# A hybrid decoder layer on one core: the rings of split weight chunks moved 128 bytes up in SBUF

## The chip, the cores and the metric

The kernel runs on one core of one Trainium2 chip. The metric is the device time of one execution in microseconds. The kernel before was timed in three runs: median 771.52 us, from 771.47 to 771.79. One further execution was recorded by the hardware profiler; its own time was 770.06 us, and from its first to its last instruction 768.3 us pass.

## The reference

One decoder layer over x of 256 tokens by 1024 channels, all in float32. Three sub-layers follow each other, each with an RMS norm ahead of it and behind it and a residual sum: a SwiGLU feed-forward of width 2816 with half weight; a mixer that runs a Mamba-2 branch (32 heads of 64, state 128, chunks of 128) beside a differential attention (8 heads) and merges the two with per-channel sigmoid gates; a second SwiGLU feed-forward.

```python
h = h + 0.5 * rmsnorm(swiglu(rmsnorm(h, g1), w_gate, w_up, w_down), g2)
z, xbc, dt, q, k, v, gates = split(rmsnorm(h, g3) @ w_in)
merged = sigmoid(gates_0) * ssd_branch(z, xbc, dt) + sigmoid(gates_1) * diff_attn_branch(q, k, v)
h = h + rmsnorm(merged @ w_out, g4)
h = h + 0.5 * rmsnorm(swiglu(rmsnorm(h, g5), w_gate2, w_up2, w_down2), g6)
```

Nearly all arithmetic is in the products with the weights, some 34 million float32 numbers that are read once.

## The kernel before, in words

**Split products.** Every large product is made from three products in a reduced float32 format: each operand is split into a high part (the operand rounded to that format) and a low part (what the rounding left), and high by high, low by high and high by low are summed. Activations are split once and stay in SBUF. Weights come in chunks of 128 partitions by 2048 numbers (1 MB, 8192 bytes in each partition). A chunk is loaded by SyncE's queue into a buffer named raw (line 217 on). ScalarE rounds it into whi (line 254), VectorE subtracts whi from raw into wlo (line 261), and TensorE multiplies with both.

**Rings.** The buffers of whi and wlo come from the function ring (line 195), one ring for each of the two. Each ring has three buffers in the pool sb, which lives as long as the kernel does. In the two feed-forward stages it has a fourth buffer in the pool of the stage: the ring counts its calls, and where the count modulo four is 3 the stage's buffer is given (line 201 on). In the mixing stage the counter still runs modulo four, but all buffers come from the three of sb. The chunks of the seven-product form of a feed-forward group (names whiq and wloq) go through the same rings. Two chunks at each border of two stages (seams, line 190) use small buffers of the stage's pool in place of the rings.

**Two kinds of products.** In mm_nat (line 386, its matmul is L395) and mm_n (line 596, L610) the weight chunk is the moving operand, 512 columns in each matmul, and a 128 by 128 block of the split activations is the stationary one. In mm_t (line 374, lines L381, L382 and L384) it is the other way round: a 128 by 128 block of whi or wlo is stationary and 256 columns of the split activations move. mm_t makes the convolution inputs, z, q and k of the mixing stage (28 chunks of 48 matmuls); the rest, both feed-forwards and the gates, branches and output of the mixing stage, is made by the other two. In a printed operand list "acc_f<-whi,gh_f" the first name behind the arrow is the moving operand.

**Order.** TensorE, ScalarE, VectorE and SyncE run in an order that is written out by hand in the feed-forwards (own_order, line 429 and 622); parts of the mixing stage are ordered by the framework, and from line 1374 on TensorE's order is by hand again. GpSimd is ordered by the framework throughout. Attention and the state-space recurrence run as background work between the matmuls of the mixing stage.

**Addresses.** Tiles of a pool lie one behind the other in the order in which their names are first used, each rounded up to 32 bytes. Pool const comes first, then sb, then the stage's pool. This is how the tiles lie in a partition of the program as it is built, in bytes; the last columns are the remainders by 256.

| tiles | pool | start before | start after the change | by 256 before | after |
|---|---|---|---|---|---|
| ident | const | 26,240 | 26,240 | 128 | 128 |
| raw, three buffers | sb | 30,624 | 30,624 | 160 | 160 |
| u0, u1 (activations of a norm, split; also o8) | sb | 55,200 | 55,200 | 160 | 160 |
| k2 (six work tiles) | sb | 71,904 | 71,904 | 224 | 224 |
| whi, three buffers | sb | 84,512 | 84,640 | 32 | 160 |
| wlo, three buffers | sb | 109,088 | 109,216 | 32 | 160 |
| small tiles | sb | 133,664 | 133,920 | | |
| stage pools: gh, gl, yh, mh, S, the fourth whi and wlo, two more raw buffers, and others | stage | 134,304 | 134,560 | 160 | 160 |

All blocks that the matmuls of whole chunks take out of these tiles start a multiple of 256 bytes from the tile's start, so the remainder of a tile is that of its operands.

Of the kernel before, what the change touches and what calls it, by code (L numbers as in the profile page):

```python
# [14 lines left out]
F32 = mybir.dt.float32  # L15
# [9 lines left out]
P = 128  # L25
T = 256
D = 1024
# [28 lines left out]
def tile_hybrid_layer(ctx: ExitStack, tc: tile.TileContext, x, ffn1_pre_g, ffn1_w_gate, ffn1_w_up,  # L56
# [4 lines left out]
    nc = tc.nc  # L61
    const = ctx.enter_context(tc.tile_pool(name="const", bufs=1))
    sb = ctx.enter_context(tc.tile_pool(name="sb", bufs=1))
# [122 lines left out]
    raws, pairs, taken, rings = [], {}, [0], {}  # L186
# [5 lines left out]
    def mixing(c):  # L192
        return mix_first <= c < mix_last

    def ring(kind, n, more, name, c, dt=F32):

        i = rings.get(kind, 0) % (n + more)
        rings[kind] = rings.get(kind, 0) + 1
        if i < n or stage[1][1] != FFN_K4 or mixing(c):
            return sb.tile([P, 2 * D], dt, tag=kind, name=name, bufs=n)  # L200
        return stage[1][0].tile([P, 2 * D], dt, tag=kind, name=name, bufs=more)

    class Raw:
# [32 lines left out]
    def blocks(name, c, nj, nc_):  # L236

        if c in seams:
            n = nj // 2
            ts = [k4([P, n, nc_], f"{name}{q}", F32R) for q in range(2)]  # L240
            return lambda j, m: ts[j // n][:, j % n:j % n + m, :]
        t = ring(name[:3], SPLIT_BUFS, SPLIT_MORE, name, c, F32R).rearrange("p (j c) -> p j c", j=nj)
        return lambda j, m: t[:, j:j + m, :]
# [226 lines left out]
    for name, v in (("mx", mix_pre_g), ("f2", ffn2_pre_g),  # L470
                    ("ng", ssd_norm_g), ("cb", ssd_conv_b), ("sg", da_subln_g)):
        n = v.shape[1] // P
# [540 lines left out]
    dt = const.tile(shp, F32, name="dt")  # L1013
# [488 lines left out]
```

## Time and profile before

| | |
|---|---|
| median of three runs | 771.52 us (771.47 to 771.79) |
| time of the profiled execution | 770.06 us |
| its span, first to last instruction | 768.3 us |
| TensorE matmul busy | 747.3 us, 97% |
| VectorE busy | 563.8 us, 73% |
| ScalarE busy | 430.8 us, 56% |
| GpSimd busy | 41.7 us, 5% |
| read from and written to HBM | 136.17 MB and 1.08 MB, 179 GB/s over the span |

The profile lists for each engine the time in which it has an instruction under way. Matmuls overlap: a matmul starts before the one ahead of it is through, and the ends are modelled, so the mean length of a matmul in a group is longer than the distance between two starts. The pace of TensorE is read from the starts.

### The profile page before, as it was taken

The page shows a single profiled execution, that of the slowest core. Times are in us where ns is not written, and L with a number is a line of the kernel's source. Part 1 is how long each engine was busy: PE and PEld are TensorE (multiplying, and loading weights), DVE is VectorE, ACT ScalarE, POOL GpSimd, SP SyncE. Part 2 cuts the span into 40 slices and gives each one's busy share as a digit, 9 for nine tenths or more (in the row PEclk, how much of TensorE's full clock was granted, in tenths as well). Part 3 has the DMA queues.
Part 4 walks back from the last instruction along what each step waited for, and adds up shares of the span by engine and source line. Part 5 has one row for each costly group of instructions (what it writes and reads, how often), then busy time and mean ns, then how long its engine had stood idle before and what let it go on. Part 6 is the DMA issues. An engine that isn't in the chain of part 4 may idle for free.

```text
span 768.3 us, 10269 instructions
## 1 busy us (share of the span) xinstructions
PE 747.3 (97%) x4113; PEld 628.5 (82%) x4113; DVE 563.8 (73%) x666; ACT 430.8 (56%) x583; POOL 41.7 (5%) x72
## 2 busy tenths in 40 slices
PE   8999899999989999999999999999999999999996
PEld 7877687788768999989999787787877888888885
DVE  6788897853557788777878878685777899987332
ACT  7543746733545555776966554774464647566321
POOL 6000000000141000000000000000012000000000
PEclk9999999999999999999999999999999999999999
DMA  9950845963355866664555564454564908458201
GB/s 324 309 194 0 275 164 169 335 208 136 103 131 177 264 188 175 188 188 141 165 180 178 151 205 140 162 165 164 165 220 164 319 10 275 162 187 334 108 1 55
DMA packets 77888, 137.92 MB, mean 179 GB/s; under 512 B 2748, under 2 KB 35600, under 8 KB 77840
## 3 DMA queue, kind: packets, MB, share of 16 engines
q1 hardware_dynamic: 75168, 129.51, 50.9%
q0 software_dynamic: 2368, 7.22, 3.2%
q8 instruction: 32, 0.52, 0.3%
q10 hardware_dynamic: 304, 0.53, 0.2%
q14 instruction: 16, 0.13, 0.1%
HBM read 136.17 MB, written 1.08 MB: 179 GB/s over the span
## 4 chain that ended last, share of the span: by engine, by line
PE 81%; DVE 7%; ACT 6%; issue 3%; POOL 1%; DMA 1%; SPq 0%; DVEq 0%; ACTq 0%; POOLq 0%
PE acc_f L610 15%; PE pu_f L395 6%; PE pg_f L395 5%; PE pws L395 5%; PE pgt L395 4%; PE pa_f L395 4%; PE pn_f L395 3%; ACT whi L254 3%; PE pwd L395 3%; DVE wlo L261 3%; PE pd_f L395 3%; PE pxs L382 2%; PE pxs L384 2%; PE pxs L381 2%; PE pz L382 2%
## 5 line engine op out<-in xcount | busy, mean ns | idle before, releaser
L261 DVE TENSOR_TENSOR wlo<-raw,whi 128x2048 fp32r<-128x2048 f32 (+2 forms) x116 | 243.5, 2109 | 96.1 <-ACT whi L254 94.0
L254 ACT CAST whi<-raw 128x2048 fp32r<-128x2048 f32 (+2 forms) x116 | 202.1, 1759 | 131.8 <-PE acc_f L610 39.5
L254 ACT CAST whiq<-raw 128x2048 fp32r<-128x2048 f32 x24 | 45.9, 1911 | 28.4 <-PE pu_f L395 11.8
L261 DVE TENSOR_TENSOR wloq<-raw,whiq 128x2048 fp32r<-128x2048 f32 x24 | 54.7, 2285 | 6.4 <-ACT whiq L254 6.4
L610 PE MATMUL acc_f<-whi,gh_f 128*128 128x512 f32 x160 | 52.3, 395 | 0.0
L610 PE MATMUL acc_f<-wlo,gh_f 128*128 128x512 f32 x160 | 52.0, 395 | 0.2 <-DVE wlo L261 0.2
L610 PE MATMUL acc_f<-whi,gl_f 128*128 128x512 f32 x160 | 52.1, 394 | 0.0
L610 PEld LDWEIGHTS acc_f<-wlo,gh_f 128*128 128x128 f32 x160 | 29.9, 188 | 7.5 <-DVE wlo L261 0.6
L610 PEld LDWEIGHTS acc_f<-whi,gl_f 128*128 128x128 f32 x160 | 30.0, 188 | 7.0
L395 PE MATMUL pgt<-whi,u_mx 128*128 128x512 f32 x128 | 35.5, 403 | 0.2 <-DVE gt L1406 0.2
L610 PEld LDWEIGHTS acc_f<-whi,gh_f 128*128 128x128 f32 x160 | 29.8, 188 | 6.8
L395 PE MATMUL pg_f<-whi,u_f 128*128 128x512 f32 x128 | 32.9, 399 | 0.9 <-DVE sg_f L768 0.9
L395 PE MATMUL pu_f<-whi,u_f 128*128 128x512 f32 x128 | 32.2, 394 | 0.0
L381 PE MATMUL pz<-u_mx,whi 128*128 128x256 f32 x128 | 31.9, 285 | 0.0
L382 PE MATMUL pz<-u_mx,whi 128*128 128x256 f32 x128 | 31.8, 285 | 0.0
L381 PE MATMUL pxs<-u_mx,whi 128*128 128x256 f32 x128 | 31.5, 284 | 0.0
L382 PE MATMUL pxs<-u_mx,whi 128*128 128x256 f32 x128 | 31.2, 282 | 0.0
L395 PEld LDWEIGHTS pg_f<-whi,u_f 128*128 128x128 f32 x128 | 23.5, 188 | 6.5 <-DVE sg_f L768 1.4
L395 PEld LDWEIGHTS pgt<-whi,u_mx 128*128 128x128 f32 x128 | 23.3, 188 | 6.6 <-issue 1.3
L395 PEld LDWEIGHTS pu_f<-whi,u_f 128*128 128x128 f32 x128 | 24.0, 188 | 5.5
L395 PE MATMUL pn_f<-whi,u_f 128*128 128x512 f32 x96 | 25.1, 395 | 0.0
L381 PEld LDWEIGHTS pz<-u_mx,whi 128*128 128x128 f32 x128 | 24.1, 189 | 0.5 <-issue 0.5
(371 smaller groups left out, 1648.3 us busy)
## 6 DMA issues: line engine op xcount, KB each, us to landing
raw<-in_w_in_dram SPq DMA_DIRECT2D x40, 1024.0 KB, 5.3
raw<-in_ffn_w_down_dram SPq DMA_DIRECT2D x22, 1024.0 KB, 5.3
raw<-in_ffn_w_gate_dram SPq DMA_DIRECT2D x18, 1024.0 KB, 5.5
raw<-in_ffn_w_up_dram SPq DMA_DIRECT2D x18, 1024.0 KB, 5.2
raw<-in_ssd_w_branch_dram SPq DMA_DIRECT2D x8, 1024.0 KB, 5.1
raw<-in_ffn_w_up_dram SPq DMA_DIRECT2D x8, 512.0 KB, 5.7
acb<-acd POOLq DMA_DIRECT2D x8, 512.0 KB, 5.0
raw<-in_da_w_branch_dram SPq DMA_DIRECT2D x4, 1024.0 KB, 5.1
```

Of the source, the lines that this page charges most:

```text
L254: i = nc.scalar.copy(got["hi"](j, step), src()[:, j:j + step, :])
L261: nc.vector.tensor_sub(got["lo"](j, step), src()[:, j:j + step, :], got["hi"](j, step).bitcast(F32))
L381: nc.tensor.matmul(acc[m], wh(j)[:, cs], ah(k0 + j), start=first and j == ks[0], stop=False)
L382: nc.tensor.matmul(acc[m], wh(j)[:, cs], al(k0 + j), start=False, stop=False)
L384: nc.tensor.matmul(acc[m], wl(j)[:, cs], ah(k0 + j), start=False, stop=last and j == ks[-1])
L395: nc.tensor.matmul(acc, a(k0 + j), b(j), start=first and i == 0, stop=last and i == 11, skip_group_check=go_on)
L610: nc.tensor.matmul(acc[b][q], x_[:, ts], w_(kt)[:, halves[q]], start=i == 0 and kt == 0 and x_ is ah and w_ is wh, stop=i == n - 1 and kt ...
```

## The change

A function gap makes a tile of 128 partitions by 32 float32 numbers (128 bytes in each partition) in pool sb and clears it with a GpSimd memset. It is called twice: just ahead of the first whi buffer and just behind the first wlo buffer. So whi and wlo start 128 bytes higher, and all that lies behind wlo, the small tiles and the stage pools, 256 bytes higher. Nothing reads the two tiles. The last byte used in a partition goes from 229,024 to 229,280.

```diff
+    def gap(name):
+        nc.gpsimd.memset(sb.tile([P, 32], F32, tag=name, name=name, bufs=1), 0.0)
+
     def ring(kind, n, more, name, c, dt=F32):
 
+        first = kind not in rings
         i = rings.get(kind, 0) % (n + more)
         rings[kind] = rings.get(kind, 0) + 1
         if i < n or stage[1][1] != FFN_K4 or mixing(c):
-            return sb.tile([P, 2 * D], dt, tag=kind, name=name, bufs=n)
+            if first and kind == "whi":
+                gap("gap0")
+            t = sb.tile([P, 2 * D], dt, tag=kind, name=name, bufs=n)
+            if first and kind == "wlo":
+                gap("gap1")
+            return t
         return stage[1][0].tile([P, 2 * D], dt, tag=kind, name=name, bufs=more)
```

## The prediction

> **What bounds the kernel now.** I read the page first: busy times, the slices over time, the chain that ended last.
>
> ```profile
> span 768.3 us, 10269 instructions
> PE 747.3 (97%) x4113; PEld 628.5 (82%) x4113; DVE 563.8 (73%) x666; ACT 430.8 (56%) x583; POOL 41.7 (5%) x72
> PE   8999899999989999999999999999999999999996
> PEclk9999999999999999999999999999999999999999
> PE 81%; DVE 7%; ACT 6%; issue 3%; POOL 1%; DMA 1%; SPq 0%; DVEq 0%; ACTq 0%; POOLq 0%
> ```
>
> TensorE is busy in nearly every slice at a full granted clock and carries 81% of the chain. So the time is set by how far apart its matmuls start. The second view is the busy time by stretches, for the place where another engine comes nearest.
>
> ```profile
> 60.00:100.00 40.00, 37.82 (x165) 29.57 (x164) 33.32 (x25) 22.07 (x17) 0.00 (x0) 1.00 0.49 159
> 260.00:320.00 60.00, 60.00 (x501) 59.67 (x500) 48.60 (x75) 32.77 (x41) 0.53 (x1) 1.00 0.62 186
> 620.00:680.00 60.00, 60.00 (x270) 48.90 (x269) 56.10 (x37) 32.91 (x29) 0.00 (x0) 1.00 0.43 146
> ```
>
> Columns: matmul, weight load, VectorE, ScalarE, GpSimd, then clock, share of the DMA engines and GB/s. Nobody else is full; VectorE reaches 56.1 of 60 us in the second feed-forward.
>
> Third, the order of time on TensorE alone, in the down projection of the first feed-forward. It has no background work and hardly a wait, and each chunk is 24 matmuls of 512 columns. The chunks that start at 157.26 and at 179.54 lie in the stage's fourth buffers (remainder 160 by 256), those that start at 162.75, 168.34 and 173.94 in the rings of sb (remainder 32). The stationary operands lie at remainder 160 throughout.
>
> ```profile
> 157.26 0.63 PE L610 MATMUL acc_f<-whi,gh_f 128*128 128x512 f32 x2
> ...
> 159.58 0.62 PE L610 MATMUL acc_f<-wlo,gh_f 128*128 128x512 f32 x2
> ...
> 162.30 0.62 PE L610 MATMUL acc_f<-wlo,gh_f 128*128 128x512 f32 x2
> 162.75 0.62 PE L610 MATMUL acc_f<-whi,gh_f 128*128 128x512 f32 x2
> ...
> 168.34 0.63 PE L610 MATMUL acc_f<-whi,gh_f 128*128 128x512 f32 x2
> ...
> 173.94 0.63 PE L610 MATMUL acc_f<-whi,gh_f 128*128 128x512 f32 x2
> ...
> 179.54 0.63 PE L610 MATMUL acc_f<-whi,gh_f 128*128 128x512 f32 x2
> 180.01 0.62 PE L610 MATMUL acc_f<-whi,gl_f 128*128 128x512 f32 x2
> ```
>
> This is what the reader is to see. From 168.34 to 179.54 there are 48 matmuls out of the rings of sb: 11.20 us, 233.3 ns each. The chunk at 157.26 takes 5.49 us to the next, 228.8 ns each; and its starts from 159.58 to 162.30, twelve matmuls, are 2.72 us apart, 226.7 ns each. Out of the stage's buffer the pace needs some ten matmuls to settle and is then 6.6 ns shorter. The same instruction with the same stationary tiles runs at two paces, by the buffer that its moving operand lies in.
>
> **The change part by part.** It adds two memsets and moves tiles; I go by what reads or writes the tiles.
>
> *Matmuls with a moving chunk.* Their number, by line (L395, then L610, over the whole span):
>
> ```profile
> 0.00:768.30 768.30, 382.92 (x1584) 1.00 0.55 180
> 0.00:768.30 768.30, 147.71 (x624) 1.00 0.55 180
> ```
>
> Of these 2208, 444 take their chunk from the stage pool (every fourth ring buffer of the feed-forwards and the seams, by the code), which leaves 1764 at remainder 32. After the change they lie at remainder 160, like the stage's buffers and like their stationary operands. In the mixing stage the pace before is a little shorter than in the down projection, as this piece of the chain of waits shows (start, length, what):
>
> ```profile
> 529.17 16.73 PE pwd L395 x72
> ```
>
> That is 232.4 ns. So the least gain is 232.4 - 228.8 = 3.6 ns and the most 233.3 - 226.7 = 6.6 ns. I take 4.7: many runs are of 12 matmuls between waits and would settle anew each time, but a chunk that follows a chunk at the same pace has nothing to settle. 1764 times 3.6, 4.7 and 6.6 ns is 6.4, **8.3** and 11.6 us.
>
> *Matmuls with a stationary chunk.* Here activations at remainder 160 move and the chunk goes from remainder 32 to 160: the two operands of a matmul differ by 128 now and agree after, as above. Their number by line (L381, L382 and L384), and a stretch of their starts:
>
> ```profile
> 0.00:768.30 768.30, 110.87 (x448) 1.00 0.55 180
> 0.00:768.30 768.30, 110.39 (x448) 1.00 0.55 180
> 0.00:768.30 768.30, 63.67 (x448) 1.00 0.55 180
> ```
>
> ```profile
> 316.04 1.11 PE L384 MATMUL pz<-u_mx,wlo 128*128 128x256 f32 x8
> 316.99 0.28 PE L381 MATMUL pz<-u_mx,whi 128*128 128x256 f32 x1
> ```
>
> Eight starts in 0.95 us, 118.8 ns each. No row shows 256 columns with both operands at the same remainder. Two bounds: nothing is gained if only the place of the moving operand counts, for that stays. If a column costs what it costs in the settled chunk, 226.7 / 512 ns, 256 columns take 113.3 ns, and 5.4 ns are to be gained. That 5.4 is close to the 5.7 (232.4 - 226.7) that 512 columns lose: the same loss for each matmul, whatever its length, is what a clash between one weight load and the stream under way would look like, and a poor place of the moving operand would not, for in mm_t it already lies at 160. So I lean to the gain, and take of it the same share as above, 4.7 of 5.7: 4.4 ns. 1344 times 4.4 is **6.0** us; the most is 7.3. As this pairing is nowhere seen, it may lose as well; I bound that by the mirror image, 7.3 us.
>
> *ScalarE and VectorE.* If the place of a tile counted for them, the split would have more than one duration, since raw, whi and wlo come from either pool:
>
> ```profile
> L261 DVE TENSOR_TENSOR wloq<-raw,whiq x24: 2280/2284/2293, 58.3 to 689.5; 128x2048 fp32r<-128x2048 f32 x24
> ```
>
> Least, median and greatest lie within 13 ns, over all pairs of buffers. I cost it at nothing, as I do the DMAs: the three raw buffers of sb stay where they are, and the others move by 256.
>
> *The two memsets.* Nearest rows (start, length):
>
> ```profile
> 0.80 0.20 POOL L445 MEMSET ident<- 128x128 f32 x1 [0.29 <-POOLq L1488]
> 0.94 0.10 POOL L449 MEMSET eps_c<- 128x1 f32 x1
> 8.89 4.15 POOL L542 TENSOR_SCALAR un_f<-h,r_f 128x512 f32<-128x512 f32 x2
> ```
>
> Each takes 0.1 to 0.2 us on an engine that is 5% busy and idles between 1.5 and 6.2 us. They cost nothing unless the framework puts both just ahead of un_f, which TensorE waits for: then 0.4 us at most.
>
> *What reaches the end.* TensorE's gain is 8.3 + 6.0 = 14.3 us. The chain runs through TensorE for 81% of 768.3 us, 622 us, of its 747.3 busy ones: 83%. Where the chain runs through VectorE and ScalarE, faster matmuls only wait longer. Some of those pieces are themselves set off by a matmul that frees a ring buffer, so I take 85%: **12.1 us**. From the profiled execution's 770.06 us that leaves 758.0; the median of the runs lies 1.46 us above that execution, so **759.4 us**. With the least and the most of the terms: 6.4 + half of 6.0 at 80% is 7.5 (764.0), and 11.6 + 7.3 at 90% is 17.0 (754.5).
>
> **The rivals.** *Only the moving operand's place counts.* Then mm_t stays at 118.8 ns, and 8.3 at 85% is 7.1 us: 764.5. For it: in the rows above the remainder of the moving operand changes and the stationary one's does not, so they cannot tell a place from an agreement of two. Against it: mm_t's excess of 5.4 ns, with its moving operand at 160.
>
> *VectorE becomes the bound in the feed-forwards.* With TensorE 2% faster its 56.1 us fall in 58.8. If the feed-forwards, with 1140 of the 1764 matmuls, kept nothing, 1140 times 4.7 at 85%, 4.6 us, is missing: 764.0. For it, waits that the list of TensorE's waits has (total, times, longest):
>
> ```profile
> PE pd_f L395 <- DVE wloq L261: 2.3, 2, 1.1
> PE pb_f L395 <- DVE wloq L261: 1.8, 2, 0.9
> ```
>
> Against it: two waits of a kind in all, and no engine above 95% even then.
>
> *Nothing changes.* The fourth buffers are faster for another reason than their remainder: they lie above 179,000 bytes in the partition, the rings below 134,000, and no row parts the two. 128 bytes then do nothing: 771.5. Against it: stationary operands of both regions go with both paces. The Trainium skill, "SBUF — State Buffer", section "Who interferes with whom", speaks for this outcome by a broader rule: TensorE has two independent read ports, one for the moving operand and one for weight loads, and never waits on anyone, so that no address should matter. The trace disagrees with that rule in so far as 233.3 and 226.7 ns stand for one instruction; by the rule the sum would be nothing.
>
> *Slower.* The stage's buffers are fast by their region, and operands that agree clash: weight load and moving stream begin at the same phase and meet from the first column. At 256 columns the load covers more of the stream, so it decides there: 1344 times 5.4 ns at 85%, 6.2 us more, 777.7. It decides as soon as mm_t's starts are over 118.8 ns apart with no gain in the 512-column matmuls. Against it: the 226.7 ns are of operands that agree.
>
> **How the numbers follow.** Forecast 0.53, only the moving operand 0.20, VectorE 0.09, nothing 0.13, slower 0.05. The range 754.5 to 768.0 holds the first three with their bounds and leaves out the last two and a little of the tails. What a measurement can tell from no change is about 0.2%, 1.5 us. Faster: 0.53 + 0.20 + 0.09 = 0.82; same 0.13; slower 0.05.
>
> **What would show it.** In the profile after: starts of the down projection's chunks 226 to 227 ns apart for all four buffers alike, with no ring buffer at 233; pwd's 72 matmuls in some 16.4 us; mm_t's eight starts in 0.91 us in place of 0.95 (0.95 again speaks for the first rival); ScalarE's and VectorE's durations as before; more idle time of TensorE ahead of wloq where it has got faster. I am wrong if the paces of the two buffers stay apart, or if they meet and the span does not follow.

## The result, and the profile after

The changed kernel takes 764.17 us (median of four runs, 763.6 to 765.81) against 771.65 us for the kernel before in the same comparison: a ratio of 0.9905, 95% interval 0.9888 to 0.9922. That is 7.5 us less by the medians and 7.3 us by the ratio. The time lies in the predicted range, 4.8 us above the point. One of the two large terms came with the opposite sign.

The page of the changed kernel (span, busy times, granted clock by slices, the chain that ended last):

```profile
span 762.5 us, 10271 instructions
PE 739.7 (97%) x4113; PEld 628.7 (82%) x4113; DVE 563.4 (74%) x666; ACT 431.3 (57%) x583; POOL 41.8 (5%) x74
PEclk9999999999999999999999999999999999999999
PE 81%; DVE 7%; ACT 6%; issue 3%; POOL 1%; DMA 1%; SPq 0%; DVEq 0%; ACTq 0%; POOLq 0%
```

TensorE's busy time falls by 7.6 us, that of the others stays within 0.5 us, the clock and the chain are as before. The instructions are the same but for the two memsets (10,271 for 10,269), and the new lines in the function move L395 to L404, L610 to L619 and L384 to L393.

The down projection in order of time on TensorE: starts of four of its chunks of 24 matmuls, of which those at 156.11 and 177.87 lie in the stage's buffers and those at 161.55 and 172.43 in the rings.

```profile
156.11 0.62 PE L619 MATMUL acc_f<-whi,gh_f 128*128 128x512 f32 x2
...
161.55 0.62 PE L619 MATMUL acc_f<-whi,gh_f 128*128 128x512 f32 x2
...
172.43 0.62 PE L619 MATMUL acc_f<-whi,gh_f 128*128 128x512 f32 x2
...
177.87 0.62 PE L619 MATMUL acc_f<-whi,gh_f 128*128 128x512 f32 x2
```

5.44 us from 156.11 to 161.55 and 10.88 us for the two chunks behind it: 226.7 ns for each matmul out of either buffer. The two paces have met, and nothing has to settle between chunks. The same in pieces of the chain of waits (start, length, what), first of the kernel before, then of the changed one; the 48 matmuls of pu_f are one chunk from the stage's buffer and one from the ring:

```profile
105.31 11.04 PE pu_f L395 x48
148.60 50.55 PE acc_f L610 x218
```

```profile
104.71 10.88 PE pu_f L404 x48
147.61 49.47 PE acc_f L619 x218
526.95 16.36 PE pwd L404 x72
```

In mm_t the starts have moved apart. From the first matmul with wlo in one half chunk to that in the next are 24 starts. Before, the first of these rows stands in the prediction (316.04) and the next is

```profile
318.89 1.11 PE L384 MATMUL pz<-u_mx,wlo 128*128 128x256 f32 x8
```

which makes 2.85 us, 118.8 ns each; after:

```profile
302.17 1.12 PE L393 MATMUL pxs<-u_mx,wlo 128*128 128x256 f32 x8
...
305.05 1.12 PE L393 MATMUL pxs<-u_mx,wlo 128*128 128x256 f32 x8
```

2.88 us, 120.0 ns each.

For a count of the whole I put each matmul of the trace beside its operands' addresses in the built program and took the distances to the next start, without those over 250 ns (512 columns) or 135 ns (256), which hold a wait or another instruction. This is what is called mean pace below. For the ring matmuls of 512 columns it goes from 232.7 to 227.7 ns, for mm_t from 118.9 to 119.8. 1764 times 5.0 less 1344 times 0.9 ns is 7.6 us, which is the fall of TensorE's busy time.

The smaller parts of the prediction: ScalarE's rounding before and after, VectorE's split after, GpSimd at the start, and TensorE's waits for VectorE.

```profile
L254 ACT CAST whiq<-raw x24: 1894/1910/1930, 53.3 to 687.4; 128x2048 fp32r<-128x2048 f32 x24
L263 ACT CAST whiq<-raw x24: 1902/1914/1932, 53.2 to 683.1; 128x2048 fp32r<-128x2048 f32 x24
L270 DVE TENSOR_TENSOR wloq<-raw,whiq x24: 2278/2284/2294, 58.2 to 685.2; 128x2048 fp32r<-128x2048 f32 x24
```

```profile
5.50 0.18 POOL L196 MEMSET gap<- 128x32 f32 x2
5.65 0.95 POOL L506 TENSOR_TENSOR r_f<-r_f,nhalf 128x1 f32<-128x1 f32 x1
8.00 0.30 POOL L505 TENSOR_SCALAR r_f<-ss_f 128x1 f32<-128x1 f32 x1 [1.41 <-DVE sq_f L542]
```

```profile
PE pd_f L404 <- DVE wloq L270: 2.3, 2, 1.2
PE pb_f L404 <- DVE wloq L270: 1.7, 2, 0.9
```

The split keeps its 2.28 us and the rounding its 1.91 us. Both memsets take 0.18 us together, ahead of 1.41 us in which GpSimd waits for VectorE. TensorE's waits for wloq are as long as they were (4.0 us in all, 4.1 before), where the prediction expected more.

### The profile page after: what moved, and what is told of

Its sections match the earlier page's. It is cut to its first block, busy times and chain, and to the rows that moved or that the text cites. A ratio compares the mean times of both kernels' runs of the same rounds, so it can differ in the third digit from the quotient of the medians.

```text
span 762.5 us, 10271 instructions
## 1 busy us (share of the span) xinstructions
PE 739.7 (97%) x4113; PEld 628.7 (82%) x4113; DVE 563.4 (74%) x666; ACT 431.3 (57%) x583; POOL 41.8 (5%) x74
## 4 chain that ended last, share of the span: by engine, by line
PE 81%; DVE 7%; ACT 6%; issue 3%; POOL 1%; DMA 1%; SPq 0%; DVEq 0%; ACTq 0%; POOLq 0%
PE acc_f L619 15%; PE pu_f L404 6%; PE pg_f L404 5%; PE pws L404 5%; PE pgt L404 4%; PE pa_f L404 4%; ACT whi L263 3%; PE pn_f L404 3%; PE pwd L404 3%; DVE wlo L270 3%; PE pd_f L404 2%; PE pz L391 2%; PE pz L390 2%; PE pz L393 2%; PE pxs L391 2%
## 5 line engine op out<-in xcount | busy, mean ns | idle before, releaser
L619 PE MATMUL acc_f<-whi,gh_f 128*128 128x512 f32 x160 | 51.6, 392 | 0.0
L619 PE MATMUL acc_f<-wlo,gh_f 128*128 128x512 f32 x160 | 51.3, 391 | 0.2 <-DVE wlo L270 0.2
L619 PE MATMUL acc_f<-whi,gl_f 128*128 128x512 f32 x160 | 51.4, 390 | 0.0
L404 PE MATMUL pgt<-whi,u_mx 128*128 128x512 f32 x128 | 35.1, 401 | 0.4 <-DVE gt L1415 0.4
L619 PEld LDWEIGHTS acc_f<-wlo,gh_f 128*128 128x128 f32 x160 | 29.9, 188 | 6.7 <-DVE wlo L270 0.6
L619 PEld LDWEIGHTS acc_f<-whi,gl_f 128*128 128x128 f32 x160 | 30.0, 188 | 6.2
L619 PEld LDWEIGHTS acc_f<-whi,gh_f 128*128 128x128 f32 x160 | 29.8, 188 | 6.2 <-ACT whi L263 0.2
L404 PE MATMUL pg_f<-whi,u_f 128*128 128x512 f32 x128 | 32.5, 397 | 1.2 <-DVE sg_f L777 1.2
L404 PE MATMUL pu_f<-whi,u_f 128*128 128x512 f32 x128 | 31.8, 391 | 0.0
L404 PEld LDWEIGHTS pg_f<-whi,u_f 128*128 128x128 f32 x128 | 23.4, 188 | 6.4 <-DVE sg_f L777 1.6
L404 PEld LDWEIGHTS pgt<-whi,u_mx 128*128 128x128 f32 x128 | 23.3, 188 | 6.4 <-issue 1.3
L404 PEld LDWEIGHTS pu_f<-whi,u_f 128*128 128x128 f32 x128 | 24.0, 188 | 5.0
L391 PEld LDWEIGHTS pz<-u_mx,whi 128*128 128x128 f32 x128 | 24.5, 192 | 0.5 <-issue 0.5
L390 PEld LDWEIGHTS pz<-u_mx,whi 128*128 128x128 f32 x128 | 24.5, 191 | 0.5 <-issue 0.5
```

The costliest lines, as they stand in the source:

```text
L390: nc.tensor.matmul(acc[m], wh(j)[:, cs], ah(k0 + j), start=first and j == ks[0], stop=False)
L391: nc.tensor.matmul(acc[m], wh(j)[:, cs], al(k0 + j), start=False, stop=False)
L404: nc.tensor.matmul(acc, a(k0 + j), b(j), start=first and i == 0, stop=last and i == 11, skip_group_check=go_on)
L619: nc.tensor.matmul(acc[b][q], x_[:, ts], w_(kt)[:, halves[q]], start=i == 0 and kt == 0 and x_ is ah and w_ is wh, stop=i == n - 1 and kt ...
```

## The experiments

The kernels differ in where three groups of tiles start: u (u0, u1 and o8), the rings, and the stage's pools. Each is given by its remainder by 256. All compute the whole layer. The diffs show the main lines only: those that set the lengths of the gaps are left out, and gap takes its length, in numbers of 4 bytes, as a second argument. In all experiments but the first the tile stage_f shares the room of another one to make space; the edit of "All at a multiple of 256" shows it.

**Place or agreement: u moved to 32, with the rings at 32 and at 160.** In the trace of before only the moving operand changed its remainder, so its place and its agreement with the stationary operand were one thing. Moving u parts them: u is stationary in pu_f, a tile of the stage is stationary in acc_f.

```diff
     def new_u(tag):
+        if uT[0] is None:
+            gap("gap_u8", 32)
# first kernel: a second gap of 128 bytes ahead of whi (rings at 32); second kernel: it lies behind wlo (rings at 160)
```

> u0, u1 and o8 are moved 128 bytes up (remainder 32 by 256), and the rings 256 bytes up in all, so that they stay at remainder 32 as in the kernel before; the stage pools stay at 160. Agreement (a matmul is quick where moving and stationary operand share the remainder by 256): the 852 matmuls whose ring chunk meets u0, u1 or o8 settle at 226.7 ns, the 912 whose ring chunk meets a tile of the stage stay near 232.7, the 252 of the stage's fourth buffers that meet u0 or u1 go from 228.6 to 233, and mm_t goes to 119.8 ns as in the changed kernel. 852 x 5 - 252 x 4.5 - 1344 x 1 ns is 1.8 us of gain: about 770. Place of the moving operand alone: all 1764 ring matmuls stay near 232.7 ns, all 444 of the stage's buffers stay quick: 771.6, but for mm_t, whose moving operand goes from 160 to 32.

> u0, u1, o8 at remainder 32, the rings and the stage pools at 160. Agreement: the 852 ring matmuls that meet u0, u1 or o8 run near 232.7 ns, and so do the 252 of the stage's buffers; the 912 that meet a tile of the stage settle at 226.7; mm_t goes back to 118.8. 912 x 5 - 252 x 4.5 ns is 3.4 us: about 768.5. Place of the moving operand alone: all 2208 matmuls of 512 columns settle at 226.7 ns as in the changed kernel, about 764.

Measured: 770.15 us for the first (ratio 0.9986, interval 0.9973 to 1.0) and 768.3 us for the second (0.996, 0.9949 to 0.9971), with the kernel before at 770.75 beside them. Pieces of the chain and two rows of the order of time of the first:

```profile
105.42 11.05 PE pu_f L405 x48
148.66 50.52 PE acc_f L622 x218
```

```profile
300.12 1.12 PE L394 MATMUL pxs<-u_mx,wlo 128*128 128x256 f32 x8
...
303.00 1.12 PE L394 MATMUL pxs<-u_mx,wlo 128*128 128x256 f32 x8
```

and of the second:

```profile
104.74 11.20 PE pu_f L405 x48
148.14 49.47 PE acc_f L622 x218
```

```profile
301.03 1.11 PE L394 MATMUL pxs<-u_mx,wlo 128*128 128x256 f32 x8
...
303.88 1.11 PE L394 MATMUL pxs<-u_mx,wlo 128*128 128x256 f32 x8
```

| kernel | u | rings | stage | pu_f x48 | acc_f x218 | 24 of mm_t |
|---|---|---|---|---|---|---|
| before | 160 | 32 | 160 | 11.04 | 50.55 | 2.85 |
| changed | 160 | 160 | 160 | 10.88 | 49.47 | 2.88 |
| first | 32 | 32 | 160 | 11.05 | 50.52 | 2.88 |
| second | 32 | 160 | 160 | 11.20 | 49.47 | 2.85 |

By its time the first kernel can't be told from no change, as its interval reaches 1.0; the second lies at the 768.5 us that agreement gave and not at 764. The paces part the two rules in both. What decides is agreement. With the rings at 160 acc_f is quick in the second kernel, as its stationary tiles are at 160 too, while both chunks of pu_f are slow (11.20 us is 233.3 ns each), the one from the stage's buffer among them, whose remainder is that of the kernel before. In the first kernel the two chunks of pu_f change parts: by mean pace the ring chunks that meet u run at 228.2 ns at remainder 32, which was the slow place before, and the stage's chunks that meet u at 232.6. mm_t goes the other way in all four: 2.88 us where u and the rings agree, 2.85 where they stand 128 apart. The rule on the moving operand's place alone has fallen.

**Other distances: rings at 64, 96, 128, and at 192, 224, 0.** Each ring buffer is 32 bytes longer, so its three buffers have three remainders; u and the stage stay at 160.

```diff
-            t = sb.tile([P, 2 * D], dt, tag=kind, name=name, bufs=n)
+            t = sb.tile([P, 2 * D + 8], dt, tag=kind, name=name, bufs=n)[:, :2 * D]
```

> Each ring buffer is 32 bytes longer, so that the three buffers of a ring start at remainders 64, 96 and 128; u0, u1 and the stage stay at 160. Agreement by 256 alone: none of the three settles at 226.7 ns; 96 and 64 lie nearer to 160 than 32 did and may lose less. A bit of 128 (same half of a 256-byte block): 64 and 96 run near 233 like 32, and 128 at 226.7 like 160. Lines of 64 bytes (a start at a multiple of 64 spares the crossing of one line): 64 and 128 are quicker than 226.7, towards 220, and 96 is not.

> As before with remainders 192, 224 and 0. Agreement by 256 alone: none at 226.7 ns. A bit of 128: 192 and 224 at 226.7, 0 near 233. Lines of 64 bytes: 192 and 0 below 226.7, 224 not. If every remainder but 32 is at 226.7, then a difference of 128 between the two operands is the one bad case.

Measured, as mean pace in ns (32 and 160 from the kernel before and the changed one; in the second row u at 160 moves and the chunk is stationary):

| remainder of the ring buffer | 32 | 64 | 96 | 128 | 160 | 192 | 224 | 0 |
|---|---|---|---|---|---|---|---|---|
| 512 columns, chunk moves | 232.7 | 234.1 | 233.2 | 233.1 | 227.7 | 233.0 | 229.9 | 233.2 |
| 256 columns, chunk stationary | 118.9 | 119.9 | 117.3 | 116.8 | 119.8 | 118.3 | 115.0 | 118.5 |

The times of one run each are 772.13 and 768.82 us. Lines of 64 bytes and halves of 256 bytes both fall: 64 and 128 are no quicker than 96, and 128 and 192 are not as quick as 160. For 512 columns agreement is the one good case, with 224 next to it. For 256 columns agreement is among the slowest, and 224, a chunk 64 above its moving operand, is the best by the mean. That mean is of two paces: seven of the ten chunks at 224 run at 113.5 to 115.2 ns and three at 117.8. At 96 it is one chunk of ten, at 113.4 ns, that runs apart from the others.

**All at a multiple of 256.** A last form of place: whether the start of a line counts once the operands agree.

```diff
# gaps of 96 bytes ahead of u, 128 ahead of whi and 128 behind wlo; a gain tile shares its room with another to make space
-    stage_f = const.tile([KD, P], F32, name="stage_f")
+    stage_f = stage_b[:KD, :]
```

> u0, u1, o8, the rings and the stage pools all start at remainder 0 by 256 (so at whole lines of 64, 128 and 256 bytes), where they all stand at 160 in the changed kernel. If the agreement of the two operands is all that counts: 226.7 ns settled for 512 columns, 120.0 for 256, and the time of the changed kernel, 764. If the place in a line counts as well: another settled pace, such as 220 ns, and 1764 x 6 ns, 10 us, less.

Measured: 765.7 us, ratio 0.9921 (0.9905 to 0.9937). The same two pieces of the chain:

```profile
104.33 10.88 PE pu_f L405 x48
147.27 49.47 PE acc_f L622 x218
```

226.7 ns again, and mm_t's 24 starts take 2.88 us (300.23 to 303.11). The changed kernel has a ratio of 0.9903 (0.9884 to 0.9921) beside the same runs of before; the intervals overlap. Where in a line both start does nothing that these runs can tell.

**Both widths at their best.** The changed kernel, in which the mixing stage's two activation tiles alone start at remainder 96. They move in mm_t and are stationary in the products for v and the gates.

```diff
-            uT[i] = sb.tile([P, 4, 2, T], F32R, tag="u8", name=f"u{i}_{tag}", bufs=2)
+            o = 48 if tag == "mx" else 0
+            t = sb.tile([P, 2 * D + 64], F32R, tag="u8", name=f"u{i}_{tag}", bufs=2)[:, o:o + 2 * D]
+            uT[i] = t.rearrange("p (j h t) -> p j h t", j=4, h=2)
```

> The changed kernel, with the two tiles of the mixing stage's activations alone (u0_mx, u1_mx) 192 bytes further on in longer buffers, remainder 96: the stationary chunk of mm_t lies 64 above its moving operand by 256. Agreement is best for both widths: mm_t goes from 119.8 towards 118 at the least and the gates' and v's 240 ring matmuls from 227.7 to 230 or more, so 763 to 765. Each width has its own best distance (the rings at 192, 224 and 0 had mm_t at 115.0 ns where the chunk stood 64 above): mm_t at 115.0, 1344 x 4.8 ns less, 240 x 2.2 ns more, of which 85% reach the end: about 759.

> The changed kernel once more on this chip, for the comparison with the others of this call: 764.2 by both theories, 0.990 of the kernel before.

Measured side by side: 759.25 us (ratio to before 0.9841, 0.9822 to 0.986) for this kernel and 764.32 (0.9903, 0.9884 to 0.9921) for the changed one, with the kernel before at 771.54. Page and order of time of the kernel with the moved activations:

```profile
span 757.7 us, 10272 instructions
PE 734.0 (97%) x4113; PEld 621.8 (82%) x4113; DVE 563.3 (74%) x666; ACT 431.4 (57%) x583; POOL 41.3 (5%) x74
```

```profile
300.03 1.07 PE L394 MATMUL pxs<-u_mx,wlo 128*128 128x256 f32 x8
...
302.75 1.07 PE L394 MATMUL pxs<-u_mx,wlo 128*128 128x256 f32 x8
```

24 starts in 2.72 us: 113.3 ns, where the changed kernel has 120.0. By mean pace mm_t goes from 119.8 to 114.4 ns, 7.3 us for 1344, and the ring matmuls that meet u_mx from 227.7 to 229.6. 5.1 us of it reach the end, as the expectation of about 759 us had it, in which each width has its own best distance. This kernel is faster than the changed one and the one before.

The difference alone does not fix the pace of 256 columns, though. Two rows of another chunk of the same kernel, at the same difference of 64:

```profile
341.65 1.11 PE L394 MATMUL pz<-u_mx,wlo 128*128 128x256 f32 x8
...
344.48 1.11 PE L394 MATMUL pz<-u_mx,wlo 128*128 128x256 f32 x8
```

24 starts in 2.83 us are 117.9 ns each. Three of mm_t's 28 chunks run at 117.8 ns and two at 116.5, the others at 113.3 to 115.3. In the changed kernel, with agreement, all 28 lie between 119.4 and 120.0. What gives a chunk its pace at a difference of 64 no run shows.

**A sweep.** Each chunk gets its own offset in a ring buffer that is 96 bytes longer.

```diff
+            o = c * 5 % 13 * 2
-            t = sb.tile([P, 2 * D], dt, tag=kind, name=name, bufs=n)
+            t = sb.tile([P, 2 * D + 24], dt, tag=kind, name=name, bufs=n)[:, o:o + 2 * D]
```

> Each weight chunk is put at its own offset in a ring buffer that is 96 bytes longer, from 0 to 96 bytes in steps of 8 by its number, so that the remainder by 256 of stationary less moving operand takes 27 values among mm_t's chunks and some 30 among the matmuls of 512 columns. No time is to be learnt from it, but the pace by the difference. If weight load and moving stream clash over the address: a smooth or stepped curve with a period of 256, for 512 columns lowest at 0 (226.7 ns) and second at 192 (229.9), for 256 columns lowest about 64 (115.0) and highest about 0 and 160 (119.8). If the changed kernel's gain had another cause than the difference, values near 0 that are not 0 (8, 16, 240, 248) would run as 0 does, or all differences alike.

Starts of chunks in the second down projection; stationary less moving operand is 136, 0, 0, 160 and 184 by 256 for the chunks that begin in these rows:

```profile
719.10 0.64 PE L621 MATMUL acc_f<-whi,gh_f 128*128 128x512 f32 x2
...
724.78 0.63 PE L621 MATMUL acc_f<-whi,gh_f 128*128 128x512 f32 x2
...
730.26 0.62 PE L621 MATMUL acc_f<-whi,gh_f 128*128 128x512 f32 x2
...
735.70 0.63 PE L621 MATMUL acc_f<-whi,gh_f 128*128 128x512 f32 x2
...
741.31 0.64 PE L621 MATMUL acc_f<-whi,gh_f 128*128 128x512 f32 x2
```

5.68 us at 136, 5.48 and 5.44 at 0 (settling, then settled), 5.61 at 160. By mean pace, 512 columns run at 229.1 ns at a difference of 0, from 231.0 (192) to 235.9 (136) at the 28 others; 16 bytes off agreement is 235.2 on one side and 231.5 on the other. So the expectation of a smooth or stepped curve did not hold for 512 columns, and that of one exact good value did. 256 columns lie between 113.9 (88) and 120.0 (112), with 119.6 at 0 and 119.7 at 160, as expected, but 117.8 at 64 where 115.0 was expected. Nearly every difference has a single chunk here, and 64 has given 113.3 as well as 117.8 ns, so the sweep can't order the differences for this width. The run took 771.97 us, from which nothing is read.

## Why the prediction was right and wrong

**Pace of the moving chunks: right, and nearly to size.** The forecast took 4.7 ns (3.6 to 6.6) off 1764 matmuls, 8.3 us; measured were 5.0 ns and 8.8 us. The reading behind it, two paces of one instruction by the remainder of its operands, was the cause. The rival that nothing changes, on grounds of another region, fell with the result itself: the ring buffers below 134,000 bytes run at 226.7 ns. By the Trainium skill's page "SBUF — State Buffer", section "Who interferes with whom", TensorE's two read ports are independent; this case's traces disagree in so far as pu_f takes 11.20 us in the second kernel and 10.88 us in the changed one, which differ for it only in where its stationary tiles start.

**Pace of mm_t: the step that failed.** "So I lean to the gain" put 4.4 ns a matmul, 6.0 us, on agreement at 256 columns. Measured were 0.9 ns more, 1.2 us lost. The step carried the good pairing of 512 columns over to 256, and took 226.7 / 512 ns a column for mm_t's pace without a clash, 113.3 ns. With agreement 256 columns settle at 120.0 ns instead. The 113.3 ns themselves are within reach, but at a difference of 64 (2.72 us for 24 starts in the kernel with the moved activations): the place was wrong, and that its figure was met elsewhere is not shown to be more than luck. The likeness of 5.4 and 5.7 ns was no evidence, since the 5.4 came out of this bound and not out of a row. The sign should have stayed open. The mirror bound there had a loss of 7.3 us, but the sum's least end took half of the gain in its place.

**The first rival's number, for another reason.** 764.5 was the price if only the moving operand's place counts. The time agrees with it, but the two kernels with u moved refute the reason: the stationary operand's place counts as much. Its sum was right by luck: mm_t's term is small for a reason that it did not know. A time alone would have confirmed a wrong rule.

**The slower rival** had the right sign for mm_t, a loss at 256 columns when the operands agree, but 5.4 ns where 0.9 were measured, and tied it to no gain at 512 columns.

**What reaches the end.** 85% was taken. TensorE's starts gained 7.6 us. The medians moved by 7.5 us here and 7.2 in the second comparison, nearly all of it, so this share was too low and made up for a little of mm_t's error; the two profiled executions by 5.85 (770.06 to 764.21), 77%. The first of them lies 1.5 us under its median, which is most of the difference. VectorE has not become the bound: TensorE waits for wloq 4.0 us in all, before the change 4.1. (The rival's "no engine above 95%" is a slip: 56.1 of its 58.8 us are 95.4%.)

**At nothing, rightly:** the two memsets (0.18 us), ScalarE's and VectorE's durations, and the DMAs, by the largest group of loads, of w_in, which land in 5.3 us at the median before and after.

**Still open** is why 512 columns are quick at exact agreement alone, and why 256 columns are not, but take one of two paces at a difference of 64. A clash of the weight load with the moving stream is an argument that fits that both operands count; no run here shows where it takes place.

## What to carry to other kernels

Where TensorE sets the pace, read the distance of its starts by buffer and not the mean of a group: a group that mixes two buffers hid 6 ns a matmul, 1% of the time. If one instruction has two paces, look at the addresses of both operands, and move one operand at a time before making a rule of it. A layout that is best for one width of matmul need not be best for another; here 256 columns did better 64 bytes apart, and giving each width its own distance was worth 5 us more than making all tiles agree.

## What the runs showed of the hardware that was not expected

With both operands at the same remainder by 256, matmuls of 512 and 256 columns in the reduced float32 format settle at 226.7 and 120.0 ns between starts, at remainders 0, 32 and 160 alike. By mean pace 512 columns take 229.6 to 235.9 ns at the other differences tried, and 256 columns 113.9 to 120.0 ns; at a difference of 64, chunks of 256 columns run at 113.3 or at 117.8 ns. At 512 columns settling takes some ten matmuls (227.7 ns by mean pace, 226.7 settled), so that short runs between waits show less than the settled gain. ScalarE's and VectorE's work on the chunks of the seven-product form does not notice: over all kernels here 1893 to 1935 ns for a rounding and 2278 to 2295 ns for a split.
